# Later first scores in two attentions, the memory's tokens turned by VectorE through DRAM, and one convolution-gate job moved, in a one-layer encoder

## The chip, the cores and the metric

The kernel runs on one core of a Trainium2 chip. The metric is device microseconds (us) for one execution; lower is better. A core has TensorE (PE in the profile: matrix products and transposes into PSUM banks), VectorE (DVE), ScalarE (ACT), GpSimd (POOL) and SyncE (SP), each with its own queue of instructions taken in order; SP, ACT and POOL also issue DMA transfers. "PEld" is PE's weight load, which overlaps its matmuls.

## The reference

One layer of an encoder over 512 tokens of 1024 channels, with 256 memory tokens. Cut to what matters here:

```python
h = rms_norm(x, norm_mix_pre)
(a_q, a_k, a_v, f_q, f_k, f_v, f_g, c_u, s_x, s_b, s_c) = split(h @ w_in, cuts)
ya = rms_norm(diff_attention(a_q, a_k, a_v, lam), diff_norm)      # 4 heads, each a difference of two softmaxes
log_f = log_sigmoid(f_g + b_fgt)
yf = forgetting_attention(f_q, f_k, f_v, log_f)                   # 8 heads, scores + cumsum(log_f) bias, causal
yc = silu(layer_norm(dwconv31(glu(c_u))))                         # convolution branch
ys = s_b * dwconv3(s_c * s_x)                                     # short convolution branch
gates = sigmoid(h @ w_gate + b_gate)                              # 4 gates of 1024 channels
mixed = sum_n(gates[n] * (branch[n] @ w_branch[n])) @ w_out
x = x + rms_norm(mixed, norm_mix_post)
m = rms_norm(mem, norm_mem)                                       # memory tokens
xk, xv = split(m @ w_xkv)                                         # cross-attention into them
x = x + rms_norm(cross_attention(rms_norm(x) @ w_xq, xk, xv) @ w_xo, norm_x_post)
x = x + rms_norm(gated_mlp_with_dwconv(x), norm_ffn_post)
```

## The kernel before

*Products.* Every large product is computed with operands split into a rounded high part and a remainder (`split`, `mm3` at line 241): three matmuls, high by high, high by low and low by high, into the same bank. All matmuls are recorded at line 232 and all PE transposes at line 238, so an instruction is told from another by its tiles. Where a tile is split, ScalarE casts the high part and VectorE subtracts it for the remainder.

*Main jobs.* `run_blocks` (line 203) takes a list of jobs. Each is a block of weights and a body. Weights are loaded three jobs ahead (tile `wr`, SP's queue) and split into `wh` (ScalarE, line 190) and `wl` (VectorE, line 191). A body with eight blocks of 128 rows is 24 matmuls of 512 columns. `mixer_jobs` (line 1143) lists the jobs of this stage in order: the two convolution branches; the gate and branch product of the short convolution; the values of the differential attention; then for each of its four heads `qk_jobs` (line 769) makes the query and the key (tile `qk`), whose remainders are VectorE's subtractions of 64 x 512 at line 783 (query) and line 792 (key, behind ScalarE's copies at lines 790 and 791), two of each, and starts the head's task. After the heads' queries and keys come 0, 2, 4 and 6 jobs of `gc`, the gate and branch jobs of the convolution branch. Then `vf_jobs` makes the forgetting attention's values and `forget_gates` (line 979) its log-forget sums (a scan at line 1005, written to DRAM as `crows` at line 1006). Then `kv_blocks(p)` makes query and key of head pair p (0 to 3) and starts its task, and after each of the pairs 1 to 3 come four jobs of `ga`, the gate and branch jobs of the differential attention. The gate's tanh is at line 1112 (tile `ge`), the product with the branch at line 1124, the addition to the accumulator at line 1125. `last_branch_jobs` (line 1276) does the same for the forgetting attention's branch, and starts `mem_task`.

*Background tasks.* The attentions run as tasks beside the main jobs. `Background` (line 47 on) holds a queue of Python generators. A task yields a pair (cost, wait): it goes on at the first tick at which the clock, an estimate of PE's work in us, has advanced by `wait`, and while credit (0.7 of PE's work, less the costs) is left. At most two tasks are stepped at a time. This happens while the program is built, so it fixes each engine's order; the framework's scheduler may move an instruction further, within the limits that `tc.issue_after(instruction)` sets.

*Differential attention, `a_task` (line 860).* Steps 0 to 3 compute the scores (`scores`, line 798) of 128, 256, 384 and 512 columns for the two softmaxes, their maxima (line 890) and exponentials, and their difference. For heads 0 to 2 ("far") the probabilities are turned key-major through DRAM: VectorE transposes squares of 32 x 32 (`turn_squares`, line 820), ScalarE's queue stores the tile (`put`, line 825), later loads it rearranged (`get`, line 833) into the low tile `ptl`, and `split_in_place` casts `pth` (line 839) and subtracts. Steps 5 and 7 begin with the products with the values (`values`, tile `ps_av`). Head 3 uses PE transposes instead.

*Forgetting attention, `f_task` (line 1016).* The same for a pair of heads, with a bias per head: `ck`, a row of `crows` broadcast to 128 partitions by GpSimd's queue (line 1024), and `fbias`, made from it by GpSimd (lines 1065 and 1067). VectorE adds bias and score and takes the maximum (line 1071); exponentials at line 1076, scales at line 1080. Pairs 0 to 2 turn through DRAM, pair 3 with PE. The end of a pair is at lines 1093 to 1096.

*Memory tokens, `mem_task` (line 1238).* For each of two tiles of 128 tokens: load (`m_t`), normalise (`normed`, into `mn`), wait 8.0, then `to_channels` (line 292): eight PE transposes into two banks, each split into 128 x 512 of `mth` and `mtl`. These are read by the key and value products of the cross-attention (`kx_jobs`, `vx_jobs`).

Of the kernel before, what the change touches and what calls it, by code (L numbers as in the profile page):

```python
# [17 lines left out]
F32 = mybir.dt.float32  # L18
F32R = mybir.dt.float32r
AF = mybir.ActivationFunctionType  # L20
ALU = mybir.AluOpType
# [4 lines left out]
P = 128  # L26
S = 512
D = 1024
# [55 lines left out]
def hybrid_layer(ctx: ExitStack, tc: tile.TileContext, a: dict, out: bass.AP):  # L84
    nc = tc.nc
    V, A, G, PE, SP = nc.vector, nc.scalar, nc.gpsimd, nc.tensor, nc.sync
# [4 lines left out]
    dram = ctx.enter_context(tc.tile_pool(name="dr", bufs=1, space=DRAM))  # L91
# [39 lines left out]
    for i in range(8):  # L131
        n = ("wh", "wl")[i % 2]
# [3 lines left out]
        elif i < 6:  # L136
            n = ("fz_raw", "fz", "fe", "fu", "fd")[i - 1]
# [61 lines left out]
        return w[k0 * P:(k0 + nk) * P, c0:c0 + n].rearrange("(k p) c -> p k c", p=P), [P, nk, n]  # L199

    bg = Background(0.7, 2)

    def run_blocks(jobs, ahead=3):

# [24 lines left out]
            bg.tick()  # L229

    def matmul(ps, lhs, rhs, start, stop):
        PE.matmul(ps, lhs, rhs, start=start, stop=stop)  # L232
        bg.clock += max(int(math.prod(rhs.shape[1:])), 256) * 0.00042

    turns = []
# [581 lines left out]
        evacuations[:] = [ins.ins]  # L817

    def turn_squares(dst, src):
        V.transpose(dst.rearrange("p (b t i) -> p b t i", b=4, i=32), src.rearrange("p (t j b) -> p b t j", b=4, j=32))  # L820

    def put(e, w):
        d = dram.tile([2, P * S], F32, tag="turned", name="turned", bufs=6)[:e.shape[1], :P * w]
# [36 lines left out]
    def a_task(h, qk, v):  # L860
        es, pt, av = {}, None, None
        far = h < 3
        for step in range(8 if far else 6):
            if step in ((5, 7) if far else (3, 5)):
                if av is None:
                    av = bank("av")
                vh, vl = (x[:, :, h * P:(h + 1) * P] for x in v[0])
                values(av, lambda kt: ((vh[:, kt], 0), (vh[:, kt], 1), (vl[:, kt], 0)), pt, step // 2 - (2 if far else 1))
            cost = 0.0
            if far:  # L870
                for qt in SPLITS.get(step, ()):
                    split_in_place(qt + 1, pt, qt % 2)
                    cost += 0.1 + 0.15 * qt
                for qt in GETS.get(step, ()):
                    if qt % 2 == 0:
                        pt = pt_tiles()
                    get(es.pop(qt)[:, 0], qt + 1, pt, qt % 2)
            elif 1 <= step <= 4:
                if step in (1, 3):
                    pt = pt_tiles()  # L880
                to_keys_major(es.pop(step - 1)[:, 0], step, pt, (step - 1) % 2)
                cost += 0.1 + 0.15 * step
            if step < 4:
                qt, w = step, (step + 1) * P
                e = es[qt] = e4()
                st = m1p.tile([P, 8], F32, tag="st8", name="st8", bufs=4)
                for c in range(2):
                    ps = bank("sc")
                    scores(ps, qk, c, qt * P, w)
                    V.tensor_tensor_reduce(e[:, c, :w], ps[:, :w], mask_a[:, S - w:], scale=1.0,  # L890
                                           scalar=-3.0e38, op0=ALU.add, op1=ALU.max,
                                           accum_out=st[:, c:c + 1])
                V.tensor_scalar(st[:, 2:4], st[:, 0:2], -HD ** -0.5, None, ALU.mult)
                for c in range(2):
                    A.activation(e[:, c, :w], e[:, c, :w], AF.Exp, bias=st[:, 2 + c:3 + c],
                                 scale=HD ** -0.5, accum_out=st[:, 4 + c:5 + c])
                V.reciprocal(st[:, 6:8], st[:, 4:6])
                V.tensor_scalar(st[:, 7:8], st[:, 7:8], lam, None, ALU.mult)
                A.activation(e[:, 1, :w], e[:, 1, :w], AF.Copy, scale=st[:, 7:8])
                V.scalar_tensor_tensor(e[:, 0, :w], e[:, 0, :w], st[:, 6:7], e[:, 1, :w], ALU.mult,  # L900
                                       ALU.subtract)
                cost += 0.6 + 0.0035 * w
                if far:
                    turn_squares(e[:, 1, :w], e[:, 0, :w])
                    es[qt] = put(e[:, 1:], w)
                    cost += 0.0015 * w
            if step == (7 if far else 5):
                e = e4()
                A.copy(e[:, 0], av)
            yield cost, 4.0 if far else 3.5  # L910

        ps = bank("tr")
        for t in range(NT):
            transpose(ps[:, t * P:(t + 1) * P], e[:, 0, t * P:(t + 1) * P])
        A.activation(e[:, 1], ps, AF.Square, scale=1.0 / math.sqrt(P))
        ms = m1p.tile([P, NT], F32, tag="ms4", name="ms4", bufs=2)
        V.tensor_reduce(ms, e[:, 1].rearrange("p (t c) -> p t c", t=NT), AX.X, ALU.add)
        r = rstd_of(m1p, [ms], NT)
        V.tensor_tensor(e[:, 0].rearrange("p (t c) -> p t c", t=NT),
                        ps.rearrange("p (t c) -> p t c", t=NT),  # L920
                        r.unsqueeze(2).to_broadcast([P, NT, P]), ALU.mult)
        yield 1.5, 3.5
        ps2 = bank("tr")
        for t in range(NT):
            transpose(ps2[:, t * P:(t + 1) * P], e[:, 0, t * P:(t + 1) * P])
        if "a" not in y:
            y["a"] = (y8b(), y8b())
        split(ps2, y["a"][0][:, h], y["a"][1][:, h], half["dn"])
        yield 0.6, 0.0
# [86 lines left out]
    def f_task(p, qk, v):  # L1016
# [5 lines left out]
        for j in range(2):  # L1022
            t = m1p.tile([P, S], F32, tag="ck", name="ck", bufs=2)
            G.dma_start(t, crows[2 * p + j:2 * p + j + 1, :].rearrange("a s -> (a s)").partition_broadcast(P))
            ck.append(t)
        yield 0.0, 2.0
        es, pts, av = {}, None, None
        for step in range(8 if far else 6):
            if step in ((5, 7) if far else (3, 5)):
                if av is None:  # L1030
                    av = [bank("av"), bank("av")]
                for j in range(2):
                    hl = v[0][:, :, 2 * p + j]
                    values(av[j], lambda kt: ((hl[:, kt], 0), (hl[:, kt], 1)), pts[j], step // 2 - (2 if far else 1))
            while step == (2 if far else 1) and f_steps[p - 1] < (8 if p - 1 < 3 else 6):
                yield 0.0, 0.5
            f_steps[p] = step + 1
# [19 lines left out]
            if step < 4:  # L1057
# [24 lines left out]
                if far:  # L1082
# [2 lines left out]
                        turn_squares(turned[:, j, :w], e[:, j, :w])  # L1085
                    es[qt] = put(turned, w)
                    cost += 0.003 * w
            yield cost, 4.5
        if "f" not in y:
            y["f"] = (y8(), y8())  # L1090

# [48 lines left out]
    def kv_blocks(p):  # L1140
        return qk_jobs(O_FQ, O_FK, p, lambda qk: bg.add(f_task(p, qk, vf), "f"))

    def mixer_jobs():
        yield from c_jobs()
        yield then(lambda: bg.add(lam_task(), "lam"))
        yield from d_jobs()
        yield then(lambda: bg.add(conv_norm_task(), "conv"))
        wide = m1p.tile([P, NT, D], F32, tag="v", name="wide")
        free = iter([wide[:, i] for i in (0, 1, 2, 3) * 2])
        ns.out_sums = out_sums = Sums(w_out, NK // 2, lambda: next(free), SP, "out_sums")  # L1150
        steps = {5: (out_sums.load, 0), 6: (out_sums.load, 1), 9: (out_sums.add, 0), 10: (out_sums.store, 0),
                 11: (out_sums.add, 1)}
        for i, job in enumerate(gate_blocks(3, "d")):
            yield job
            if i in steps:
                yield then(lambda f=steps[i]: f[0](f[1]))
        yield then(lambda: y.pop("d"))
        vj = v_jobs(O_AV, va)
        yield then(lambda: (out_sums.store(1), out_sums.load(2), out_sums.load(3)) and None)
        for f, q in ((out_sums.add, 2), (out_sums.add, 3)):  # L1160
            yield next(vj)
            yield then(lambda f=f, q=q: f(q))
            yield then(lambda q=q: out_sums.store(q))
        yield from vj
        yield share(False)
        gc = gate_blocks(2, "c")
        for h, n in enumerate((0, 2, 4, 6)):
            yield from qk_jobs(O_AQ, O_AK, h, lambda qk, h=h: bg.add(a_task(h, qk, va), "a"))
            if n:
                yield then(lambda: bg.drain("conv"))  # L1170
            for _ in range(n):
                yield next(gc)
        yield then(lambda: bg.drain("a"))
        yield from vf_jobs(vf)
        yield from kv_blocks(0)
        ga = gate_blocks(0, "a")
        for p in range(1, 4):
            yield from kv_blocks(p)
            for _ in range(4):
                yield next(ga)  # L1180
        yield then(lambda: bg.drain("f"))

# [55 lines left out]
    def mem_task():  # L1238
        for t in range(2):
            m_t = stage("s1", "m_t")  # L1240
            G.dma_start(m_t, mem_d[t * P:(t + 1) * P, :])
            y_t = normed(ns.xm, m_t, [ns.gain], stage("s2", "mn"))
            if t == 0:
                space(ns.xm, "gap8", 96)
            yield 1.3, 8.0
            to_channels(y_t, ns.mt, t)
            yield 1.2, 0.0

    def kx_jobs():
# [577 lines left out]
```

## Time and profile before

| | |
|---|---|
| median of three runs | 1061.24 us |
| lowest and highest | 1059.8 and 1061.26 us |
| the profiled execution: its own time | 1061.52 us |
| the profiled execution: its span | 1059.7 us |
| mean granted PE clock | 0.996 |
| data moved by DMA | 164.37 MB |

The span is the time from the first to the last instruction or transfer in the trace; the execution's own time is measured around it. One line of a timeline gives the start in us, the duration, engine, source line, operation, out<-in by tile name, size and count, and in brackets the idle time in front with who ended it. A line of the list of waits gives who waited, on whom, the total in us, how many times, and the longest. A line of a window view gives the window, its length, then the busy time of PE, PEld, DVE, ACT and POOL with the number of instructions, then the granted PE clock as a share of full speed, the share of time that the DMA engines were busy, and GB/s. A line of groups gives line, engine, operation, tiles, shape and count, then busy us and mean ns of one, then idle time in front. Matmuls overlap in PE's pipeline, so the durations of PE's rows add up to more than the time between their starts.

### The profile page before, as it was taken

What the parts mean: (1) busy time and instruction counts of PE and PEld (TensorE: products, weight loads), DVE (VectorE), ACT (ScalarE), POOL (GpSimd) and SP (SyncE); (2) the same over time, 40 slices, a digit from 0 to 9 for tenths busy, and PEclk for the clock granted to TensorE, in tenths of its full rate; (3) what the DMA queues carried; (4) which work ended last, traced back from release to release, by engine and by line L of the source; (5) the groups of instructions that cost most, each with busy time, mean ns of one, the idle gap of its engine ahead of it and who ended that gap; (6) DMA issues with size and microseconds to landing.
All of it is one profiled execution on the core that took longest, in us unless ns stands there. A gap on an engine that the chain in (4) does not pass through costs nothing.

```text
span 1059.7 us, 14521 instructions
## 1 busy us (share of the span) xinstructions
PE 1045.3 (99%) x5279; PEld 886.9 (84%) x5279; DVE 806.2 (76%) x1277; ACT 499.7 (47%) x820; POOL 144.7 (14%) x246
## 2 busy tenths in 40 slices
PE   9999999999999999999999999999999999999997
PEld 7888888888888987887878899999888888888886
DVE  6999997568677368787676888886768677667796
ACT  5322222367555355644543665654333333445672
POOL 4000000000000014322110031031111211111001
PEclk9999999999999999999999999999999999999999
DMA  7954333324333245565335743226576676725662
GB/s 260 314 159 96 108 89 100 99 83 141 115 103 108 56 124 173 170 189 145 100 113 177 268 137 119 81 79 193 185 247 214 215 230 213 232 80 179 211 217 79
DMA packets 186109, 164.37 MB, mean 155 GB/s; under 512 B 20352, under 2 KB 158061, under 8 KB 186038
## 3 DMA queue, kind: packets, MB, share of 16 engines
q1 hardware_dynamic: 152995, 119.91, 37.4%
q10 hardware_dynamic: 30482, 35.01, 10.0%
q0 software_dynamic: 2560, 8.54, 2.5%
q8 instruction: 41, 0.67, 0.3%
q14 instruction: 31, 0.25, 0.1%
HBM read 139.69 MB, written 23.74 MB: 154 GB/s over the span
## 4 chain that ended last, share of the span: by engine, by line
PE 89%; issue 4%; DVE 4%; DMA 2%; ACT 1%; POOL 0%; ACTq 0%; SPq 0%; POOLq 0%; DVEq 0%
PE ps_mm L232 46%; PE ps_av L232 29%; PE ps_sc L232 7%; PE ps_tr L232 4%; PE ps_tr L238 2%; DVE wl L191 1%; DMA e<-in_w_in 1%; PE ps_mm L450 1%; PE ps_av L450 1%; DVE e L820 0%; DVE e L1071 0%; ACT e L1076 0%; DMA ck<-crows 0%; DVE e L890 0%; DVE qk L792 0%
## 5 line engine op out<-in xcount | busy, mean ns | idle before, releaser
L190 ACT CAST wh<-wr 128x1024 fp32r<-128x1024 f32 (+1 forms) x140 | 146.7, 1049 | 271.1 <-PE ps_mm L232 154.2
L191 DVE TENSOR_TENSOR wl<-wr,wh 128x1024 fp32r<-128x1024 f32 (+1 forms) x140 | 175.6, 1255 | 104.9 <-ACT wh L190 104.8
L232 PE MATMUL ps_mm<-hth,wh 128*128 128x512 f32 (+1 forms) x616 | 231.0, 381 | 1.0 <-DVE qk L792 0.9
L232 PE MATMUL ps_mm<-htl,wh 128*128 128x512 f32 (+1 forms) x616 | 229.7, 379 | 0.0
L232 PE MATMUL ps_mm<-hth,wl 128*128 128x512 f32 (+1 forms) x616 | 229.4, 379 | 0.0
L232 PEld LDWEIGHTS ps_mm<-hth,wh 128*128 128x128 f32 x616 | 114.3, 188 | 22.4 <-PE ps_sc L232 1.4
L232 PEld LDWEIGHTS ps_mm<-hth,wl 128*128 128x128 f32 x616 | 113.9, 188 | 21.5
L232 PEld LDWEIGHTS ps_mm<-htl,wh 128*128 128x128 f32 x616 | 114.2, 188 | 20.3
L232 PE MATMUL ps_av<-htl,wh 128*128 128x512 f32 (+1 forms) x328 | 122.6, 374 | 0.0
L232 PE MATMUL ps_av<-hth,wh 128*128 128x512 f32 (+1 forms) x328 | 122.5, 374 | 0.0
L232 PE MATMUL ps_av<-hth,wl 128*128 128x512 f32 (+1 forms) x328 | 122.5, 374 | 0.0
L682 DVE SCALAR_TENSOR_TENSOR y<-y,par,y 128x508 f32<-128x508 f32 (+29 forms) x120 | 83.1, 736 | 0.1
L232 PEld LDWEIGHTS ps_av<-hth,wl 128*128 128x128 f32 x328 | 61.7, 188 | 11.0
L232 PEld LDWEIGHTS ps_av<-htl,wh 128*128 128x128 f32 x328 | 61.5, 188 | 10.9
L232 PEld LDWEIGHTS ps_av<-hth,wh 128*128 128x128 f32 x328 | 61.6, 188 | 10.7
L1618 DVE TENSOR_TENSOR wl<-dw,wh 128x1024 fp32r<-128x1024 f32 x32 | 40.1, 1258 | 15.0 <-ACT wh L1617 14.8
L1617 ACT CAST wh<-dw 128x1024 fp32r<-128x1024 f32 x32 | 33.5, 1052 | 22.4 <-PE ps_tr L232 7.9
L1565 ACT ACTIVATE th<-c 128x512 f32<-128x512 f32 x22 | 13.9, 632 | 48.9 <-DVE c L612 48.9
L1065 POOL TENSOR_SCALAR fbias<-ck,cq 128x128 f32<-128x128 f32 (+3 forms) x32 | 22.9, 722 | 78.0 <-DVE st L1071 72.5
L612 DVE SCALAR_TENSOR_TENSOR c<-ps_mm,par,c 128x510 f32<-128x510 f32 (+1 forms) x44 | 32.7, 744 | 0.7
L232 PE MATMUL ps_mm<-y8b,wh 128*128 128x512 f32 x96 | 30.9, 402 | 0.8 <-DVE ge L1124 0.8
L232 PE MATMUL ps_mm<-y,wh 128*128 128x512 f32 x96 | 30.5, 396 | 0.2 <-DVE ge L1124 0.2
(479 smaller groups left out, 2091.8 us busy)
## 6 DMA issues: line engine op xcount, KB each, us to landing
wr<-in_w_up SPq DMA_DIRECT2D x44, 512.0 KB
wr<-in_w_in SPq DMA_DIRECT2D x38, 512.0 KB
wr<-in_w_gate SPq DMA_DIRECT2D x32, 512.0 KB
wp<-in_w_down ACTq DMA_DIRECT2D x22, 512.0 KB
sums<-wp ACTq DMA_DIRECT2D x22, 512.0 KB
dw<-sums SPq DMA_DIRECT2D x44, 256.0 KB
wr<-in_w_branch SPq DMA_DIRECT2D x16, 512.0 KB
wide<-in_w_out SPq DMA_DIRECT2D x12, 512.0 KB
```

Source lines behind the costliest of these rows:

```text
L190: order(A.copy(hi, raw[:, :n]))
L191: low.tensor_tensor(lo, raw[:, :n], hi.bitcast(F32), ALU.subtract)
L232: PE.matmul(ps, lhs, rhs, start=start, stop=stop)
L238: turns.append(PE.transpose(ps, x, ident[:n, :n]).ins)
L450: keep(PE.matmul(banks[c][:, :S // 2], w[p == 1][:, k, c * P:(c + 1) * P], ht[p == 2][:, i * 4 + k, :S // 2], start=(i, p, k) == (0, 0, 0) ...
L612: ins = V.scalar_tensor_tensor(dst[:, s:], src[:, :S - s], w(k), dst[:, s:], ALU.mult, ALU.add)
L682: ins = V.scalar_tensor_tensor(dst[:, s:], src[:, :S - s], pc("conv_dw", k * 4 + j), dst[:, s:], ALU.mult, ALU.add)
L1065: G.tensor_scalar(bias[:, :w], ck[j][:, :w], -1.0, cq[:, qt, head:head + 1], ALU.mult, ALU.add)
L1565: A.activation(th, c[:, 0], AF.Silu)
L1617: A.copy(hi, x)
L1618: V.tensor_tensor(lo, x, hi.bitcast(F32), ALU.subtract)
```

## The change

Five edits:

- `matmul` records the last PE matmul in `steps_of`. The products with the values of far heads and pairs are put behind the matmul that was last at the time (`tc.issue_after(steps_of[0])`).
- Before its first step a head's task waits 3.0 (before: nothing), and a pair's task 5.0 instead of 2.0.
- After step 5 of a far head or pair, the wait is 6.0 instead of 4.0, or 6.5 instead of 4.5.
- `mem_task` turns its tokens with VectorE and DRAM in place of the PE transposes: four transposes of squares, 128 x 512 each, for the two tiles, into `m_t`; a store to DRAM; after a wait of 13.0 four loads per tile, rearranged, into `mtl`; after a further 8.0 one cast into `mth` and one subtraction, 128 x 1024 each. The wait after normalising is 5.0 instead of 8.0.
- The convolution branch has 5 instead of 6 jobs behind the fourth head; its last job follows the query and key of the forgetting attention's pair 0. The differential attention's gate jobs behind pairs 1, 2 and 3 are 3, 4 and 5 (before: 4 each).

```diff
@@ -199,6 +199,7 @@
         return w[k0 * P:(k0 + nk) * P, c0:c0 + n].rearrange("(k p) c -> p k c", p=P), [P, nk, n]
 
     bg = Background(0.7, 2)
+    steps_of = []
 
     def run_blocks(jobs, ahead=3):
 
@@ -229,7 +230,7 @@
             bg.tick()
 
     def matmul(ps, lhs, rhs, start, stop):
-        PE.matmul(ps, lhs, rhs, start=start, stop=stop)
+        steps_of[:] = [PE.matmul(ps, lhs, rhs, start=start, stop=stop).ins]
         bg.clock += max(int(math.prod(rhs.shape[1:])), 256) * 0.00042
 
     turns = []
@@ -817,7 +818,9 @@
         evacuations[:] = [ins.ins]
 
     def turn_squares(dst, src):
-        V.transpose(dst.rearrange("p (b t i) -> p b t i", b=4, i=32), src.rearrange("p (t j b) -> p b t j", b=4, j=32))
+        if len(dst.shape) == 2:
+            dst = dst.rearrange("p (b t i) -> p b t i", b=4, i=32)
+        V.transpose(dst, src.rearrange("p (t j b) -> p b t j", b=4, j=32))
 
     def put(e, w):
         d = dram.tile([2, P * S], F32, tag="turned", name="turned", bufs=6)[:e.shape[1], :P * w]
@@ -860,12 +863,15 @@
     def a_task(h, qk, v):
         es, pt, av = {}, None, None
         far = h < 3
+        yield 0.0, 3.0
         for step in range(8 if far else 6):
             if step in ((5, 7) if far else (3, 5)):
                 if av is None:
                     av = bank("av")
                 vh, vl = (x[:, :, h * P:(h + 1) * P] for x in v[0])
-                values(av, lambda kt: ((vh[:, kt], 0), (vh[:, kt], 1), (vl[:, kt], 0)), pt, step // 2 - (2 if far else 1))
+                with tc.issue_after(steps_of[0]) if far else ExitStack():
+                    values(av, lambda kt: ((vh[:, kt], 0), (vh[:, kt], 1), (vl[:, kt], 0)), pt,
+                           step // 2 - (2 if far else 1))
             cost = 0.0
             if far:
                 for qt in SPLITS.get(step, ()):
@@ -907,7 +913,7 @@
             if step == (7 if far else 5):
                 e = e4()
                 A.copy(e[:, 0], av)
-            yield cost, 4.0 if far else 3.5
+            yield cost, (6.0 if step == 5 else 4.0) if far else 3.5
 
         ps = bank("tr")
         for t in range(NT):
@@ -1023,15 +1029,17 @@
             t = m1p.tile([P, S], F32, tag="ck", name="ck", bufs=2)
             G.dma_start(t, crows[2 * p + j:2 * p + j + 1, :].rearrange("a s -> (a s)").partition_broadcast(P))
             ck.append(t)
-        yield 0.0, 2.0
+        yield 0.0, 5.0
         es, pts, av = {}, None, None
         for step in range(8 if far else 6):
             if step in ((5, 7) if far else (3, 5)):
                 if av is None:
                     av = [bank("av"), bank("av")]
-                for j in range(2):
-                    hl = v[0][:, :, 2 * p + j]
-                    values(av[j], lambda kt: ((hl[:, kt], 0), (hl[:, kt], 1)), pts[j], step // 2 - (2 if far else 1))
+                with tc.issue_after(steps_of[0]) if far else ExitStack():
+                    for j in range(2):
+                        hl = v[0][:, :, 2 * p + j]
+                        values(av[j], lambda kt: ((hl[:, kt], 0), (hl[:, kt], 1)), pts[j],
+                               step // 2 - (2 if far else 1))
             while step == (2 if far else 1) and f_steps[p - 1] < (8 if p - 1 < 3 else 6):
                 yield 0.0, 0.5
             f_steps[p] = step + 1
@@ -1085,7 +1093,7 @@
                         turn_squares(turned[:, j, :w], e[:, j, :w])
                     es[qt] = put(turned, w)
                     cost += 0.003 * w
-            yield cost, 4.5
+            yield cost, 6.5 if far and step == 5 else 4.5
         if "f" not in y:
             y["f"] = (y8(), y8())
 
@@ -1164,7 +1172,7 @@
         yield from vj
         yield share(False)
         gc = gate_blocks(2, "c")
-        for h, n in enumerate((0, 2, 4, 6)):
+        for h, n in enumerate((0, 2, 4, 5)):
             yield from qk_jobs(O_AQ, O_AK, h, lambda qk, h=h: bg.add(a_task(h, qk, va), "a"))
             if n:
                 yield then(lambda: bg.drain("conv"))
@@ -1173,10 +1181,11 @@
         yield then(lambda: bg.drain("a"))
         yield from vf_jobs(vf)
         yield from kv_blocks(0)
+        yield from gc
         ga = gate_blocks(0, "a")
         for p in range(1, 4):
             yield from kv_blocks(p)
-            for _ in range(4):
+            for _ in range(2 + p):
                 yield next(ga)
         yield then(lambda: bg.drain("f"))
 
@@ -1242,8 +1251,24 @@
             y_t = normed(ns.xm, m_t, [ns.gain], stage("s2", "mn"))
             if t == 0:
                 space(ns.xm, "gap8", 96)
-            yield 1.3, 8.0
-            to_channels(y_t, ns.mt, t)
+            yield 1.3, 5.0
+            for i in range(2):
+                turn_squares(m_t.rearrange("p (b t i) -> p b t i", b=4, i=32)[:, :, 4 * i:4 * i + 4],
+                             y_t[:, i * S:(i + 1) * S])
+                yield 1.0, 0.0
+            d = dram.tile([P * D], F32, tag="turned_m", name="turned_m", bufs=2)
+            A.dma_start(d.rearrange("(p x) -> p x", p=P), m_t)
+            yield 0.0, 13.0
+            hi, lo = (x[:, :, t * P:(t + 1) * P] for x in ns.mt)
+            raw = lo.bitcast(F32)
+            src = d.rearrange("(a j b k i) -> a (j b) k i", a=4, j=32, b=4, i=32)
+            for a_ in range(4):
+                with tc.issue_after(evacuations[0]):
+                    A.dma_start(raw[:, :, 32 * a_:32 * a_ + 32], src[a_])
+            yield 0.0, 8.0
+            with tc.issue_after(evacuations[0]):
+                A.copy(hi, raw)
+            V.tensor_tensor(lo, raw, hi.bitcast(F32), ALU.subtract)
             yield 1.2, 0.0
 
     def kx_jobs():
```

## The prediction

> **What bounds the kernel now.** I read the page's busy times and chain of waits, then the list of TensorE's (PE's) waits, then PE's timeline at each.
>
> ```profile
> span 1059.7 us, 14521 instructions
> ...
> PE 1045.3 (99%) x5279; PEld 886.9 (84%) x5279; DVE 806.2 (76%) x1277; ACT 499.7 (47%) x820; POOL 144.7 (14%) x246
> ...
> PE 89%; issue 4%; DVE 4%; DMA 2%; ACT 1%; POOL 0%; ACTq 0%; SPq 0%; POOLq 0%; DVEq 0%
> ```
>
> PE is busy for 99% of the span and is 89% of the chain. So an edit gains if it takes instructions off PE or closes a gap in its stream, and what it adds to another engine costs nothing until PE has to wait for it. The gaps, as who waits for whom (total, times, longest):
>
> ```profile
> PE ps_sc L232 <- DVE qk L792: 1.2, 1, 1.2
> PE ps_mm L232 <- DVE ge L1124: 1.0, 2, 0.8
> PE ps_av L232 <- DVE e L1095: 0.9, 1, 0.9
> PE ps_mm L232 <- DVE qk L792: 0.9, 1, 0.9
> PE ps_av L232 <- ACT pth L839: 0.8, 1, 0.8
> PE ps_sc L232 <- ACT qk L791: 0.6, 1, 0.6
> ```
>
> The tiles (qk, ge, pth, e) are those of the two attentions and of the gate jobs run beside them. The worst place is the first score of the forgetting attention's last pair. PE's rows overlap, so I measure from start to start:
>
> ```profile
> 478.09 0.22 PE L232 MATMUL ps_sc<-qk 128*128 128x128 f32 x1
> 479.49 0.30 PE L232 MATMUL ps_sc<-qk 128*128 128x128 f32 x1 [1.18 <-DVE qk L792]
> 480.59 0.73 PE L232 MATMUL ps_mm<-y8b,wh 128*128 128x512 f32 x2 [0.81 <-DVE ge L1124]
> ...
> 482.19 1.05 PE L232 MATMUL ps_mm<-y8b,wh 128*128 128x512 f32 x2
> 483.04 0.63 PE L232 MATMUL ps_mm<-y8b,wl 128*128 128x512 f32 x1
> ```
>
> The score is asked for before VectorE has written the key's remainder (line 792): 1.40 us where a 128-column score takes about 0.1 (the row of four at 446.51, in a fence below). Behind it a matmul waits for a bank that the late VectorE empties (line 1124): 1.10 us. After these two, matmuls of 512 columns take (483.04 - 482.19)/2 = 0.43 us, where the transposes' fence below shows 0.23. The window view gives the reason in its clock column (third from the right):
>
> ```profile
> 480.60:485.00 4.40, 4.40 (x14) 3.50 (x15) 4.31 (x11) 2.48 (x7) 0.22 (x1) 0.65 0.62 157
> ```
>
> A mean clock of 0.65 over 4.40 us is 4.40 x 0.35 = 1.5 us lost. So this one late score costs 1.3 + 1.0 + 1.5 = 3.8 us.
>
> **The change part by part.** The order of both built programs is known; from it I count instructions. Nothing moves ahead of the differential attention's second head, and nothing after the last branch.
>
> *Memory's tokens.* Sixteen transposes leave PE, eight for each tile of 128 tokens.
>
> ```profile
> 547.38 0.40 PE L232 MATMUL ps_mm<-hth,wl 128*128 128x512 f32 x1
> 547.61 1.04 PE L238 MATMUL ps_tr<-ident,mn 128*128 128x128 f32 x8
> 548.40 0.48 PE L232 MATMUL ps_mm<-hth,wh 128*128 128x512 f32 x1
> 548.72 0.40 PE L232 MATMUL ps_mm<-htl,wh 128*128 128x512 f32 x1
> ```
>
> Eight hold PE for 548.40 - 547.61 = 0.79 us, and the matmul behind them starts its successor 0.32 us later instead of 0.23: 0.88 together. Two groups: **-1.7 us** (bounds -1.6 and -1.8). In their place VectorE gets four 128x512 turns of squares and ScalarE's queue two stores and eight loads of 128 KB in pieces of 128 bytes; four half-size splits become two whole ones. The attention does the same today:
>
> ```profile
> 397.44 0.37 ACTq L825 DMA_DIRECT2D turned<-e  x1
> ...
> 399.49 0.93 ACTq L833 DMA_DIRECT2D ptl<-turned  x2
> ...
> 403.20 0.74 ACT L839 CAST pth<-ptl 128x128 fp32r<-128x128 f32 x2
> ```
>
> A store was followed by its loads 2.05 us later; 128 KB in such pieces was in place 3.71 us after issue at the most. Four times that, 14.8 us, bounds one tile's loads, 2 to 4 us its store. In the built order PE reads the tokens' second half over 40 us of its work after their loads are issued. The loads wait in ScalarE's queue for the store, with a gate's tanh and a weight cast behind; their first readers on PE stand some 10 us of matmuls later. The copy and the remainder wait for the loads with VectorE's sum for a gate behind, read about 13 us of matmuls later. I cost both at nothing; uncovered, each us of lateness is a us. The bound on a loss is 14.8 + 4 - 13 = 6 us, the bound on a further gain nothing, since PE has no wait there today.
>
> [...]
>
> *First scores later.* Between a key's last matmul and the head's first score the built order now has, in 512-column matmuls, 45 instead of 24 for the second head, 24 (and 14 small ones) instead of 12 for the third, and 48 instead of 12 for the last pair. The third head today:
>
> ```profile
> 265.54 0.33 PE L232 MATMUL ps_sc<-qk 128*128 128x128 f32 x2
> 266.45 0.30 PE L232 MATMUL ps_sc<-qk 128*128 128x128 f32 x1 [0.58 <-ACT qk L791]
> 266.96 0.73 PE L232 MATMUL ps_mm<-y,wh 128*128 128x512 f32 x2 [0.21 <-DVE ge L1124]
> ```
>
> 0.91 us for two scores and 0.51 for one, about 1.1 above 0.1 each. With 12 more matmuls (2.7 us) ahead both go: **-1.1 us** (bounds 0 and -1.1). At the last pair 36 more are 8 us: **-3.8 us** (bounds 0 and -3.8).
>
> *Values behind the latest matmul, a longer wait at step 5.* For the second pair they move from behind the third pair's scores to 36 matmuls after them:
>
> ```profile
> 446.51 0.56 PE L232 MATMUL ps_sc<-qk 128*128 128x128 f32 x4
> 446.91 0.33 PE L232 MATMUL ps_av<-pth,v 128*128 128x256 f32 x1
> 448.01 0.39 PE L232 MATMUL ps_av<-pth,v 128*128 128x256 f32 x1 [0.77 <-ACT pth L839]
> 448.43 0.39 PE L232 MATMUL ps_av<-ptl,v 128*128 128x256 f32 x1
> ```
>
> 1.10 and 0.42 us where 0.12 is usual (256 columns, half of 0.23): **-1.3 us** (bounds 0 and -1.3).
>
> *The first pair, and the moved job.* The 24 matmuls of the last branch-convolution job now stand between this pair's key and the next query, and bring VectorE two sums and two additions. This is where I expect a loss. The chain begins at the turn of the log-forget values, after which PE goes on at 381.35:
>
> ```profile
> 381.35 0.48 PE L232 MATMUL ps_mm<-hth,wl 128*128 128x512 f32 x1
> ...
> 401.53 0.47 PE L232 MATMUL ps_mm<-hth,wh 128*128 128x512 f32 x1 [0.88 <-DVE qk L792]
> ```
> ```profile
> 382.27 1.22 DVE L191 TENSOR_TENSOR wl<-wr,wh 128x1024 fp32r<-128x1024 f32 x1 [1.18 <-ACT wh L190]
> ...
> 392.78 0.29 DVE L1071 CUSTOM_DVE_ANT_0 e<-ps_sc,fbias 128x128 f32<-128x128 f32 x1 [2.67 <-POOL fbias L1067]
> ...
> 400.68 0.69 DVE L792 TENSOR_TENSOR qk<-ps_mm,qk 64x512 fp32r<-64x512 f32 x1 [0.70 <-ACT qk L791]
> ```
> ```profile
> L191 DVE TENSOR_TENSOR wl<-wr,wh 128x1024 fp32r<-128x1024 f32 x44 | 54.8, 1245 | 26.7 <-ACT wh L190 26.7
> L820 DVE STREAM_TRANSPOSE e<-e 128x384 f32<-128x384 f32 x9 | 7.4, 851 | 0.0
> L820 DVE STREAM_TRANSPOSE e<-e 128x256 f32<-128x256 f32 x9 | 5.4, 621 | 0.1
> ```
>
> Today VectorE gets its first bias at 392.78, 11.4 us after 381.35, and ends the next pair's second key remainder at 401.37, 8.6 us later: 20.0 us, and PE, whose wait is 0.88, is held. In the new order the weight remainder of 382.27 (1.2) no longer stands ahead of the scan, so the first part is 10.2 us. In the second part VectorE's queue has, ahead of that key remainder, two more weight remainders (2.5), one more query remainder and an addition (2 x 0.69), two turns of 256 (1.2) and two of 384 (1.7), and the scales, maxima and small ones of these two steps, some 2.8 by what is left of today's 8.6 us for one such step: 9.6 more, 18.2 in all, so 28.4. PE has between the same points 102 matmuls of 0.23 and 16 scores, about 102 x 0.23 + 16 x 0.15 = 25.9 us. VectorE is late by 2.5 us, or 1.6 if its instructions overlap as PE's rows do by some 0.05 each; I take 2.0, against 0.9 now: **+1.1 us** (bounds -0.9, no wait, and +3.1: 2.5 and a low clock of 1.5).
>
> *New short waits.* In the new order eight places have 12 matmuls or fewer between a producer's input and its reader (gate sums, value splits, the last head's copies). Today such places wait between 0 and 0.8. I take half of them at 0.4: **+1.6 us** (bounds 0 and 8 x 0.8 = 6.4).
>
> Sum: -1.7 - 1.1 - 3.8 - 1.3 + 1.1 + 1.6 = -5.2. The profiled execution took 1061.52 us (1.8 of it around the span), so 1056.3; the median of the runs is 0.3 lower: **1056.0 us**.
>
> **The rivals.**
> - *Low clock at the first pair.* A wait of 1.18 and 0.81 lowered the clock at 480; that of 0.88 at 401.53 did not, by the clock of 1.00 behind it:
>
> ```profile
> 401.00:405.00 4.00, 3.47 (x15) 2.93 (x16) 3.63 (x11) 2.76 (x8) 1.19 (x3) 1.00 0.52 124
> ```
>
>   At 2.0 it is open: 1056.0 + 1.5, with 0.5 for the wait's upper end: 1058.0. [...]
> - *The stalls only move* (the scores come later, and so do the sums they delay): the transposes alone remain, 1061.2 - 1.7 = 1059.5. For it: VectorE is loaded where all waits lie. Against it: the last pair's gain is 36 matmuls of slack, not a shift by three.
> - *No new wait at all*: 1056.0 - 2.0 - 1.6 = 1052.4, and 1051 with the other small waits of today.
> - *Slower: VectorE stays late after the first pair.* Its queue there cannot make up 2.5 us before the next pair, so the same wait with its low clock (4.0) comes at the next two pairs, and the last pair's 3.8 stays: 1061.2 - 1.7 - 1.1 + 3.1 - 1.3 + 4.0 = 1064.2. It decides once VectorE is still over 2 us late when pair 2's scores begin. Against it: between the pairs stand 24 to 36 gate matmuls (5 to 8 us) whose VectorE work is two sums.
>
> **How the numbers follow.** Forecast 0.62, low clock 0.13, stalls move 0.10, no new wait 0.09, slower 0.06. Less than 0.2% (2.1 us, from 1059.1 to 1063.4) can't be told from no change. The forecast, no new wait and most of the low clock lie under it: faster 0.83. Stalls that move are "same", with the rest of the low clock: 0.11. Slower 0.06. The range of 8 in 10 goes from 1052.0 (no new wait) to 1060.0 (the stalls move, with 0.5 for a new one).
>
> **What would show it.** Right: no transposes of mn on PE and none of its waits on the memory copies; no wait over 0.5 us at the first scores of the third head and the last pair; clock 1.00 in the windows of the last pair; a wait of 1.5 to 2.5 us for qk's remainder beside the first pair. Wrong: a mean clock under 1 in the first pair's windows, waits on pth or ge that add to more than 3 us, or a PE wait on mth or mtl.

## The result, and the profile after

The changed kernel took 1067.34 us (median of 4 runs, 1065.71 to 1068.25) against 1061.23 us (4 runs): the ratio is 1.0059, with an interval of 1.0046 to 1.0071. It is 6.1 us slower where 5.2 us faster was forecast. The profiled execution took 1066.76 us. In all that follows one execution of the fifth experiment, which ran at a mean clock of 0.654 and took 1491.36 us, is left out.

The page of the changed kernel, its busy times and the chain that ended last:

```profile
span 1065.0 us, 14506 instructions
...
PE 1042.1 (98%) x5263; PEld 884.8 (83%) x5263; DVE 808.7 (76%) x1279; ACT 500.5 (47%) x818; POOL 144.4 (14%) x246
...
PE 92%; DVE 3%; DMA 2%; issue 1%; ACT 1%; ACTq 0%; POOL 0%; DVEq 0%; POOLq 0%; SPq 0%
```

PE is busy for 3.2 us less than before, and the span is 5.3 us longer, so PE stands idle somewhere. The list of PE's waits (who waits on whom, total, times, longest) names the place:

```profile
PE ps_mm L233 <- DVE ge L1132: 8.4, 2, 7.8
PE ps_mm L233 <- DVE qk L793: 1.8, 1, 1.8
...
PE ps_av L233 <- ACT e L915: 0.7, 1, 0.7
```

One wait of 7.8 us on a gate sum (line 1132 is line 1124 of before). PE's timeline there:

```profile
578.26 0.39 PE L233 MATMUL ps_mm<-wh,mix 128*128 128x512 f32 x1
586.47 0.80 PE L233 MATMUL ps_mm<-wh,mix 128*128 128x512 f32 x1 [7.82 <-DVE ge L1132]
587.06 0.63 PE L233 MATMUL ps_mm<-wl,mix 128*128 128x512 f32 x1
...
591.30 0.39 PE L233 MATMUL ps_av<-wh,mix 128*128 128x512 f32 x1
```

From 578.26 to the next start 8.21 us go by where 0.23 is the pace: 8.0 lost. Then 11 matmuls take 591.30 - 586.47 = 4.8 us instead of 11 x 0.23 = 2.5: the clock is low (0.50 in the window from 586 to 590) and costs 2.3 more. Together 10.3 us. The chain of waits between 566 and 592 says what PE waited for, in order of time:

```profile
572.28 11.13 DMA mtl<-turned_m
...
583.51 1.05 ACT mth L1270
...
584.59 1.23 DVE mtl L1271
585.82 0.61 DVE ge L1132
...
586.47 1.65 PE ps_mm L233 x3
```

Read backwards: PE needs a bank that VectorE's gate sum empties; that sum stands in VectorE's queue behind the remainder of the memory's second tile; the remainder needs the cast; the cast needs the last of the four loads of turned tokens, which landed 11.1 us after its issue. On ScalarE:

```profile
561.54 0.35 ACTq L1260 DMA_DIRECT2D turned_m<-m_t  x1
...
567.38 1.06 ACT L158 ACTIVATE mix<-mix 128x1024 fp32r<-128x1024 f32 x1 [4.25 <-DVE mix L587]
567.88 0.55 ACTq L1267 DMA_DIRECT2D mtl<-turned_m  x1
...
583.51 1.04 ACT L1270 CAST mth<-mtl 128x1024 fp32r<-128x1024 f32 x1 [8.73 <-DMA wide<-out_sums]
```

The store was issued at 561.54, the first load 6.3 us later, and 15.6 us after that the cast began. What stands directly ahead of the first load is ScalarE's copy of `mix` (line 158), for which ScalarE had waited 4.25 us on VectorE. The bracket names a transfer of SP's queue that ended at the same moment; the chain names the load itself.

Ahead of this place the kernel had gained. The same matmul, the first behind the last pair's values, starts at 531.16 before and at 528.03 after:

```profile
531.16 0.73 PE L232 MATMUL ps_av<-y,wh 128*128 128x512 f32 x2 [0.93 <-DVE e L1095]
```
```profile
528.03 0.73 PE L233 MATMUL ps_av<-y,wh 128*128 128x512 f32 x2 [0.93 <-DVE e L1103]
```

So 3.1 us were won by 528, and 1.8 with the sixteen transposes behind it (the first matmul from `mix` starts at 580.03 before and at 575.09 after, 4.9 us earlier); 10.3 were lost at 578. That is +5.4, and the profiled executions differ by 1066.76 - 1061.52 = 5.2 us. Of the 3.1, 0.3 is older than the first changed instruction: one and the same matmul near 100 us starts at 100.33 before and at 100.01 after.

```profile
100.33 0.39 PE L232 MATMUL ps_av<-hth,wh 128*128 128x512 f32 x1
```
```profile
100.01 0.39 PE L233 MATMUL ps_av<-hth,wh 128*128 128x512 f32 x1
```

### The profile page after: what moved, and what is told of

It reads as the page before. It is cut to its first block, busy times and chain, and to the rows that moved or that the text cites. A ratio compares the mean times of both kernels' runs of the same rounds, so it can differ in the third digit from the quotient of the medians.

```text
span 1065.0 us, 14506 instructions
## 1 busy us (share of the span) xinstructions
PE 1042.1 (98%) x5263; PEld 884.8 (83%) x5263; DVE 808.7 (76%) x1279; ACT 500.5 (47%) x818; POOL 144.4 (14%) x246
## 4 chain that ended last, share of the span: by engine, by line
PE 92%; DVE 3%; DMA 2%; issue 1%; ACT 1%; ACTq 0%; POOL 0%; DVEq 0%; POOLq 0%; SPq 0%
PE ps_mm L233 50%; PE ps_av L233 28%; PE ps_sc L233 7%; PE ps_tr L233 4%; PE ps_tr L239 2%; DMA mtl<-turned_m 2%; PE ps_mm L451 1%; PE ps_av L451 1%; DVE wl L191 0%; DMA xs<-in_x 0%; ACTq L1267 0%; DVE ge L1132 0%; DVE m_t L823 0%; DVE e L823 0%; DMA turned_m<-m_t 0%
## 5 line engine op out<-in xcount | busy, mean ns | idle before, releaser
L233 PEld LDWEIGHTS ps_av<-hth,wl 128*128 128x128 f32 x328 | 61.6, 188 | 10.7
L1643 DVE TENSOR_TENSOR wl<-dw,wh 128x1024 fp32r<-128x1024 f32 x32 | 40.1, 1257 | 15.5 <-ACT wh L1642 15.3
```

The costliest lines, as they stand in the source:

```text
L233: steps_of[:] = [PE.matmul(ps, lhs, rhs, start=start, stop=stop).ins]
L1643: V.tensor_tensor(lo, x, hi.bitcast(F32), ALU.subtract)
```

## The experiments

Ratios are to the kernel before, run again beside the experiments: its medians were 1060.74 us for the first four, 1060.93 for the next four and 1060.76 for the last three.

Theory A: the whole loss is the second tile's loads, late by their small pieces and by what runs beside them, with the gate sum queued behind them. Rivals: VectorE is late there anyway (B); the small pieces hold up other transfers on which PE waits (C).

**The memory part undone** (`mem_task` of before in the changed kernel).

> The changed kernel with the memory's tokens turned by PE again; its four other edits stay. Theory A (late loads): the whole loss is the second tile's four loads, for which ScalarE waits 8.7 us and PE 7.8, with 2.0 lost to the low clock behind it, 10.3 in all between 560 and 600 us; the other edits had gained 3.1 us by 560. So 1061.2 - 3.1 = 1058.1 us, with no PE wait over 1 us behind 560. Rival B (busy VectorE): the gate sums would be late at that place however the tokens are turned, because VectorE comes late out of the attentions; then 1064 us or more and a PE wait on ge stays.

Measured: 1059.21 us (10 runs, 1058.17 to 1060.61), ratio to the kernel before 0.9985 (0.9976 to 0.9995). PE's longest wait on ge is 0.6 us. B falls. That it is 1.1 us above the 1058.1 expected has a cause of its own. The ten runs lie in two groups, 1058.2 to 1058.7 and 1059.7 to 1060.6; the profiled one is of the upper:

```profile
400.01 1.07 PE L233 MATMUL ps_sc<-qk 128*128 128x512 f32 x4
403.12 0.47 PE L233 MATMUL ps_mm<-hth,wh 128*128 128x512 f32 x1 [2.05 <-DVE qk L793]
```
```profile
404.00:408.00 4.00, 4.00 (x13) 3.09 (x12) 2.38 (x8) 1.83 (x6) 2.11 (x4) 0.58 0.69 185
```

Behind the first pair's wait of 2.05 us the clock is 0.58 for 4 us (third column from the right), 1.7 us lost. Only this execution has a trace; the mean clocks fit the same reading for the others, 0.996 or 0.997 in the upper group and 0.998 or 0.999 in the lower. In the changed kernel's profile the wait was 1.77 us and the clock stayed at 1.00:

```profile
403.07 0.47 PE L233 MATMUL ps_mm<-hth,wh 128*128 128x512 f32 x1 [1.77 <-DVE qk L793]
```
```profile
404.00:408.00 4.00, 4.00 (x20) 3.27 (x19) 2.38 (x8) 2.12 (x6) 1.86 (x4) 1.00 0.71 189
```

**The memory part alone** (the new `mem_task` in the kernel before).

> The kernel before, with the memory part of the change alone. Theory A: 1061.2 + 10.3 - 1.8 (sixteen transposes less) = 1069.7 us, slower than the whole change, with a PE wait on ge of 7 to 9 us. Rival B: the wait needs the shifted attentions, so here it is under 2 us: 1059.5 to 1062 us.

Measured: 1069.34 us (4 runs), ratio 1.0077 (1.0061 to 1.0093), with a longest wait of PE on ge of 6.3 us. The wait is shorter than the 7 to 9 expected; behind it the clock is 0.50 until about 592 and 0.72 from 592 to 596, which costs some 3 us. So the loss comes with this part, whatever the attentions do.

**The second tile's remainder later.**

```diff
-            with tc.issue_after(evacuations[0]):
-                A.copy(hi, raw)
-            V.tensor_tensor(lo, raw, hi.bitcast(F32), ALU.subtract)
+            if t == 1:
+                ns.rest = hi, lo, raw
+                return
...
+            if n == 7:
+                A.copy(hi, raws[n])
+                v = V.tensor_tensor(lo, raws[n], hi.bitcast(F32), ALU.subtract)
+                mh, ml, mr = ns.rest
+                with tc.issue_after(v.ins):
+                    A.copy(mh, mr)
+                    V.tensor_tensor(ml, mr, mh.bitcast(F32), ALU.subtract)
```

> The changed kernel with only the second tile's copy and remainder put behind the eighth weight split of the output projection; the loads stay where they are. Theory A as a matter of order (the late loads cost only because the copy stands ahead of ScalarE's casts and the remainder ahead of VectorE's gate sums): the wait goes, 1067.3 - 10.3 = 1057.0 us, and the loads still land 10 us or more after their last issue. Rival C (the transfers themselves): the small pieces hold up the weight loads of the output projection that share the DMA engines, so PE waits for those weights instead: 1061 us or more.

Measured: 1068.84 us (10 runs, 1061.3 to 1070.66), ratio 1.0064 (1.0042 to 1.0086). This decided nothing: the limit was set on VectorE's instruction, and ScalarE's copy moved forward (with a limit on ScalarE's own instruction, in the fifth run, it stayed behind):

```profile
572.75 0.70 ACTq L1267 DMA_DIRECT2D mtl<-turned_m  x1
585.88 1.04 ACT L1384 CAST mth<-mtl 128x1024 fp32r<-128x1024 f32 x1 [15.49 <-DMA mtl<-turned_m]
586.84 1.04 ACT L155 CAST wh<-wr 128x1024 fp32r<-128x1024 f32 x1
```

The cast now stood ahead of a weight cast too, ScalarE waited 15.5 us for the loads, and PE 10.7. Two of the ten executions took only 1061.3 us; they have no trace.

**Whole rows** (the same loads, unturned: this kernel leaves out the turn, so it does not compute the layer).

```diff
-                    A.dma_start(raw[:, :, 32 * a_:32 * a_ + 32], src[a_])
+                    A.dma_start(raw[:, 2 * a_:2 * a_ + 2], rows[:, 2 * a_:2 * a_ + 2])
```

> The changed kernel with the four loads per tile read back unturned, in pieces of 1 KB in place of 128 bytes: the same bytes, queue, order and waits, but the memory's tokens stay unturned. Theory A1 (number of pieces): each load is 1024 pieces of 128 bytes now and 128 pieces of 1 KB then, so it lands within 6 us of its issue and the wait on ge is under 1 us: about 1057 us. Theory A2 (bytes in a crowd): the DMA engines are over 90% busy from 570 to 580 whatever the pieces, so the loads still land past 580 and 1064 us or more remain.

Measured: 1056.67 us in one run. The longest wait on ge is 0.6 us. The loads were issued from 566.31 and the cast ran at 572.43, 6.1 us later instead of 15.6. From 568 to 570 and from 570 to 572, when these pieces moved, the DMA engines were about as busy as in the changed kernel (0.76 and 0.95 against 0.74 and 1.03). So the number of pieces is a necessary part of the cause.

**Both copies later** (`issue_after` set for each on its own engine; the cut is against the third run).

```diff
-                with tc.issue_after(v.ins):
+                with tc.issue_after(c.ins):
                     A.copy(mh, mr)
+                with tc.issue_after(v.ins):
                     V.tensor_tensor(ml, mr, mh.bitcast(F32), ALU.subtract)
```

> As the third run, with the copy held on ScalarE too: in that run the copy had moved ahead of a weight cast and a tanh on ScalarE, and only the remainder had moved back on VectorE, so it did not tell order from transfers. Now both stand behind the eighth weight split of the output projection on their own engines. Theory A (order): PE no longer waits for the gate sum, 1057 to 1058.5 us, while the loads still land past 580. Theory C (transfers): the weight loads on SP's queue that run beside the small pieces are late themselves (in the changed kernel three of them took 5.3 us to issue at 573), so PE waits for weights near 580: 1061 us or more.

Measured: 1058.6 us (9 runs, 1056.26 to 1060.78), ratio 0.9981 (0.9971 to 0.999), at the upper edge of what was expected. PE's longest wait on ge is 0.6 us, and PE's timeline in the profiled execution (1057.11 us) has no marked wait between 560 and 620, though the pieces are as small as before: order is the other part of the cause, and C falls. Two things differ from what was expected. The loads are not past 580: all 4160 packets of ScalarE's queue start before it. And the median is 1.4 us above that of the next run, which no trace explains.

**Pieces of 1 KB.**

```diff
-            hi, lo = (x[:, :, t * P:(t + 1) * P] for x in ns.mt)
-            raw = lo.bitcast(F32)
+            hi, lo = (x[:, :, t * P:(t + 1) * P].rearrange("p k (a i) -> p a k i", a=4) for x in ns.mt)
+            raw = stage("s2", "raw").rearrange("p (a k i) -> p a k i", a=4, k=NK)
...
-                    A.dma_start(raw[:, :, 32 * a_:32 * a_ + 32], src[a_])
+                    A.dma_start(raw[:, a_], src[a_])
```

> The changed kernel with the loads' target in the order of the pieces in DRAM (1 KB a piece, as in the fourth run), in the buffer that the normalised tokens have left; the cast and the remainder put the tokens in channel order as they write. It computes what the reference does. Theory A1 (number of pieces): 1056.7 us as in the fourth run, up to 1058.3 where the low clock of the first pair joins in; no PE wait over 1 us behind 560. Rival: casts that read one order and write another are slow, so that the gate sum behind them is late: over 1060 us.

Measured: 1057.19 us (8 runs, 1056.34 to 1059.78), ratio 0.9973 (0.9962 to 0.9983): faster than both kernels. The second tile's loads are issued from 569.37 and the cast runs at 577.18, 7.8 us later; PE does not wait there. The runs lie in two groups here too, five up to 1057.4 and three from 1058.5; the profiled one (1058.53) is of the upper, with a wait of 2.33 us at the first pair and a clock of 0.64 behind it.

**Without the moved jobs** (the sixth kernel with gate jobs 0, 2, 4, 6 and 4, 4, 4).

> The sixth run's kernel with the convolution's job back behind the fourth head and four gate jobs behind each pair. Theory D (the moved job makes VectorE late at the first pair): the wait for the key's remainder falls from 2.0 to about 1 us and no execution has the low clock there: 1 to 2 us faster than the sixth run, 1055.5 to 1056.5 us. Rival E (the job covers more than it costs): the first scores of the pairs lose their cover and the waits on qk or ge come back: 1058 us or more.

Measured: 1057.58 us (10 runs), ratio 0.9975 (0.9966 to 0.9984), no better than the sixth run and between the two theories. The wait at the first pair did fall to 1.1 us, but others came:

```profile
PE ps_mm L233 <- DVE ge L1132: 2.0, 3, 0.8
...
PE ps_tr L239 <- DVE ptl L156: 1.3, 1, 1.3
PE ps_mm L233 <- DVE qk L793: 1.1, 1, 1.1
```

**Without the longer waits in front of the first scores.**

> The sixth run's kernel without the two longer waits in front of the first scores (nothing for a head, 2.0 for a pair, as before). Theory F (the waits close the gaps of the third head and the last pair, 1.1 and 3.8 us): 1061 to 1062 us, with PE waits on qk at about 266 and 480 and a clock under 1 behind 480. Rival: the moved jobs and the values behind the latest matmul do it, and the waits are worth under 1 us: below 1058 us.

Measured: 1058.93 us (10 runs), ratio 0.9988 (0.9979 to 0.9998): 1.7 us above the sixth run, between the two theories. The wait at the third head is back (0.6 us on qk, at 266), and the longest wait on a gate's tanh is 1.4 us (0.7 in the sixth run). At the last pair none came back:

```profile
483.52 0.56 PE L233 MATMUL ps_sc<-qk 128*128 128x128 f32 x4
```

With the gate jobs moved, or with the longer wait (the seventh run), the last pair's gap is closed; either will do.

**The loads of x later** (small pieces stay).

```diff
             ns.x[t] = ns.work.tile([P, D], F32, tag="xin", name="xin", bufs=2)
+            if t < 2:
+                G.tensor_copy(ns.x[t][:, 0:1], ns.mt[0][:, 0, P:P + 1].bitcast(F32))
```

> The changed kernel, small pieces as they are, but GpSimd's two loads of x (512 KB each) wait for the second tile's cast, through a copy of one column from it. In the changed kernel all but 65 of the second tile's 4096 pieces had started by 580, and the last ones start in windows in which GpSimd's loads take 95% and 72% of the DMA engines. Theory A2 (the crowd delays the pieces): the cast starts at about 580.5 instead of 583.5 us, PE waits 4 to 5 us instead of 7.8, 1063 to 1065 us. Theory A1 alone (the pieces take their time whatever runs beside them): the cast stays within 1 us of 583.5, 1066 to 1068 us.

Measured: 1063.44 us (10 runs, 1060.91 to 1065.21), ratio 1.0025 (1.0016 to 1.0034). In the profiled execution, the longest of the ten (1065.21 us), the cast began 13.5 us after the first load's issue at 568.25 instead of 15.6, and PE waited 5.8 us instead of 7.8. This is less than A2 expected and more than A1 allows: the crowd counts as well, and this edit took only a part of it away. The changed kernel's DMA queues from 572 to 576 and from 576 to 580 (packets, MB, share of the 16 engines; q10 is ScalarE's, q1 SP's, q0 GpSimd's):

```profile
q1 hardware_dynamic: 1235, 0.91, 80.9%
q10 hardware_dynamic: 898, 0.11, 18.1%
```
```profile
q1 hardware_dynamic: 495, 0.90, 62.6%
q10 hardware_dynamic: 1574, 0.20, 31.8%
q0 software_dynamic: 71, 0.28, 17.2%
```

The shares add up to 99% and 112% of the 16 engines' time (at 112% the times of some packets overlap), so next to none of it is free, and the small pieces get 18.1% and 31.8%. In the second window all three queues move data.

**The 1 KB memory part alone**, in the kernel before.

> The kernel before with the memory part of the change alone, its loads in pieces of 1 KB as in the sixth run. By theory A the transposes' 1.7 us remain as a gain and nothing else moves: 1060.9 - 1.7 = 1059.2 us. Rival: the second tile's copy is still late enough in this order to cost 1 us or more: 1060.2 us or more.

Measured: 1059.33 us (10 runs), ratio 0.9987 (0.9978 to 0.9997): 1.4 us less than the 1060.76 beside it. The transposes' gain is there once the loads are in time.

**The convolution's job one pair later**, in the sixth kernel.

```diff
         yield from kv_blocks(0)
-        yield from gc
         ga = gate_blocks(0, "a")
         for p in range(1, 4):
             yield from kv_blocks(p)
+            if p == 1:
+                yield from gc
```

> The sixth run's kernel with the convolution's last job behind the second pair's query and key instead of the first pair's. Theory D (VectorE is late at the first pair because of that job): the wait at 404 falls under 1 us and the low clock with it, 1055.5 to 1056.5 us. Rival E2 (as the seventh run: VectorE is late by about the same total wherever the job stands, and the waits only move): 1057 to 1058 us.

Measured: 1056.56 us (5 runs, 1056.22 to 1056.82), ratio 0.9962 (0.9948 to 0.9976): the lowest median of the complete kernels, 4.2 us under the 1060.76 beside it, though its interval overlaps the sixth run's. It has no wait on qk in the list; a wait of 1.6 us on a gate sum at 393.76 takes its place:

```profile
393.76 0.73 PE L233 MATMUL ps_mm<-y,wh 128*128 128x512 f32 x2 [1.60 <-DVE ge L1132]
```

All five runs lie within 0.6 us, without the second group. So D is right on the low clock, and E2 in part: some lateness only moved.

## Why the prediction was wrong

The step that failed is the costing of the memory's loads: "I cost both at nothing". The prediction had a bound on the loss beside it, 14.8 + 4 - 13 = 6 us, larger than the whole forecast gain, and gives no reason for taking the other end; no rival was made of the bound, and the range took in none of it. Measured on the second tile, term by term:

- *Loads, 14.8 us as a bound.* 15.6 us from the first issue to the cast. That the size fits is luck. The bound took four times the 3.71 us from 399.49 to 403.20 before, as if the parts came one after another, and in that time the engines were busy to 0.78 only. The first tile's four loads are of the same form, and ScalarE's cast stood behind other work and did not wait for them:

```profile
547.10 5.18 ACTq L1267 DMA_DIRECT2D mtl<-turned_m  x4
...
557.42 1.04 ACT L1270 CAST mth<-mtl 128x1024 fp32r<-128x1024 f32 x1
```

  4058 of the 4160 packets of ScalarE's queue had started by 554, 6.9 us after the first issue; from 552 to 554 it had the engines nearly to itself (2874 of the 2881 packets). So "nothing" held for the first tile. The second tile's loads met full engines, as the windows from 572 to 580 show (99% and 112%).
- *Store, 4 us as a bound.* 6.3 us from its issue to the first load's; the chain runs through ScalarE's wait for VectorE there, not through the store.
- *Cover, 13 us of matmuls.* From the store's issue at 561.54 to PE's stop at 578.49 it was 17.0 us, of which 10.6 lay behind the first load's issue.
- *What follows the landing, not counted.* Cast, remainder, gate sum: 583.51 to 586.47, 3.0 us, each waiting for the one ahead.
- *The low clock behind it, not counted here*, though it was for the last pair: 2.3 us.

6.3 + 15.6 + 3.0 - 17.0 = 7.9 (8.0 without rounding), and 2.3 make the 10.3 us, above the bound of 6 as well.

Every sign that the prediction gave for being right came out: no waits on the memory's PE copies, none at the first scores of the third head and the last pair, a clock of 1.00 at the last pair, and a wait of 1.77 us beside the first pair. Of its signs of being wrong one came too, waits on ge of more than 3 us (8.4).

The rest, by its own steps:

- *Transposes, -1.7:* right for the instructions that leave PE, 1.8 in the profile and 1.4 in the tenth run; the part as a whole cost 8.6 us as built (second run).
- *Third head, -1.1:* right; its wait is gone in the profile after, and came back in the eighth run.
- *Last pair, -3.8:* mostly right in size and in mechanism, as this fence shows.

```profile
480.89 0.56 PE L233 MATMUL ps_sc<-qk 128*128 128x128 f32 x4
482.03 0.50 PE L233 MATMUL ps_mm<-hth,wh 128*128 128x512 f32 x1 [0.59 <-DVE ge L1132]
```
```profile
478.00:484.00 6.00, 5.41 (x26) 4.41 (x25) 5.96 (x15) 3.38 (x7) 2.84 (x4) 1.00 0.71 197
```

  The four scores and the gap behind them take 1.14 us, 0.7 over their pace, and the clock is 1.00: about 3.1 us are won. The matmuls between key and scores did not need the longer wait (eighth run): the moved jobs put them there as well, and the prediction did not tell the two edits apart.
- *Second pair's values, -1.3:* the wait on pth is gone from the list.
- *First pair, +1.1:* right; the wait is 1.77 us in the profile after against 0.88, and 2.04 to 2.33 in the profiles of the first, third to sixth and ninth runs. Its low clock, a rival at 0.13, did not show in the profile after; it did in those of the first and the sixth run, and by the mean clocks in half of the first run's executions.
- *New short waits, +1.6:* of the right kind: three places waited about 0.7 us, where four at 0.4 were taken. One is the 0.59 on ge just shown, which the line above already counts; the others are the values of the last head (0.67) and the gate ahead of 445.39 (0.71):

```profile
348.59 0.39 PE L233 MATMUL ps_av<-wh,hth 128*128 128x264 f32 x1 [0.67 <-ACT e L915]
```
```profile
445.39 0.73 PE L233 MATMUL ps_mm<-y8b,wh 128*128 128x512 f32 x2 [0.71 <-ACT ge L1120]
```

  All steps but the transposes came to -3.5 in the sum, and to -3.1 by the matmul at 528.03, or -2.8 without what was there at 100 us. Apart from the memory's loads the sum held; it failed by that one term.
- *The slower rival* put a lasting lateness of VectorE at the pairs. VectorE did make it up there (the list above has one wait on qk); the loss had another place, so that this rival forecast a slower kernel is luck.

## What to carry to other kernels

A transfer that replaces work on the bound engine has to be costed with the DMA traffic of its own stage (the cast began 13.5 instead of 15.6 us after the first load's issue with part of that traffic moved) and with the whole chain behind its landing (3.0 us here), and the instruction that waits for it belongs behind everything urgent on its engine (1058.6 us in the fifth run against 1067.34). Where the bound of a term is larger than the whole forecast gain, the term is a rival with a chance, not a nought. It paid to store turned data so that its pieces come back long: the same tokens in pieces of 1 KB took the whole change from 6.1 us slower to 3.7 faster (1057.19 against 1060.93 beside it).

## What the runs showed of the hardware

How much of the DMA engines the turned loads took is read from ScalarE's queue. In the changed kernel, from 570 to 572 and from 580 to 583 (between them lie the two windows shown above):

```profile
q10 hardware_dynamic: 1623, 0.21, 65.6%
```
```profile
q10 hardware_dynamic: 65, 0.01, 1.7%
```

4160 packets, nearly all pieces of 128 bytes, took 2 x 0.656 + 4 x 0.181 + 4 x 0.318 + 3 x 0.017 = 3.4 us of all 16 engines, 13 ns for one piece on one engine. In the sixth run, in pieces of 1 KB, from 570 to 576 and from 576 to 580:

```profile
q10 hardware_dynamic: 534, 0.49, 24.5%
```
```profile
q10 hardware_dynamic: 42, 0.04, 2.6%
```

That is 6 x 0.245 + 4 x 0.026 = 1.6 us for the same tokens, less than half of the 3.4 us that the pieces of 128 bytes took.

Behind the single wait of PE at the first pair the clock was low in some profiles and not in others: 0.58 behind 2.05 us in the first experiment and 0.64 behind 2.33 in the sixth, but not lowered behind 2.04, 2.10, 2.11 and 2.23 in the third, fourth, ninth and fifth. So the length alone did not decide here. Behind the fourth run's wait the window view has a clock of 1.00:

```profile
404.00:408.00 4.00, 4.00 (x19) 3.28 (x18) 2.41 (x7) 2.12 (x6) 2.11 (x4) 1.00 0.65 181
```

What else decided was not tried.
